# Stick-breaking attention: one 1408-column tile for a head's three score pieces

## The chip, the cores and the metric

The kernel runs on one core of a Trainium2 chip. The time is device microseconds of one execution; several executions are timed and the median is given. One execution was also recorded by the hardware profiler, and every row below comes from it.

## What is computed

The program is a two-layer diffusion block followed by a second block; the change concerns one part of the second: stick-breaking attention with 8 heads of 64 over 512 positions. Cut to that part, the reference is:

```python
def stick_breaking_attention(q, k, v):      # one block of queries
    z = einsum('bhqd,bhkd->bhqk', qb, kh) * scale
    mask = key_pos[None, :] < q_pos[:, None]
    log_1mb = where(mask, log_sigmoid(-z), 0.0)
    later = cumsum(log_1mb, axis=3, reverse=True) - log_1mb
    w = where(mask, exp(log_sigmoid(z) + later), 0.0)
    return einsum('bhqk,bhkd->bhqd', w, vh)
```

The kernel uses that -log_sigmoid(-z) is softplus(z) = max(z, 0) + ln(1 + exp(-|z|)).

## The kernel before

Scores stand with keys on the partitions. A head has four key tiles of 128; of the queries only those that can see the keys are kept, so key tile 0 has 512 columns, key tile 1 has 384, key tiles 2 and 3 have 256 each and share one bank. These three pieces (512, 384, 512 columns: indices 0, 1, 2) are three PSUM banks `Z`.

`sb_prep` (line 1624) makes a head's queries and keys: transposes (lines 1630 and 1634), a ScalarE copy (1637) and VectorE subtractions (1638, 1644). `sb_scores` (line 1651) issues 12 matmuls (lines 1656 to 1658) in the order of key tiles 2, 3, 1, 0, then for each piece in the order 2, 0, 1: the absolute value (ScalarE, 1664), exponential and logarithm (ScalarE through the helper of line 210, in place in tile `t`), max and add (VectorE, 1667), and `split` (lines 345 and 346): a cast to `hi` and a subtraction that gives `lo` (tiles `p`, VectorE). So a head has 9 ScalarE and 9 VectorE instructions here.

`sb_weights` (line 1753) adds the running sums to the scores in place: 20 matmuls (line 1760) with `hi` and `lo` of the pieces as the moving operand, beginning with key tile 3, which lies in piece 2; then three exponentials from `Z` to tiles `w`, which free the score banks. `sb_out` (line 1768) makes the output of a pair of heads from `w` (line 1774).

TensorE's instructions of the stage are in a scheduled order written out by hand:

```python
for h in range(9):
    if h < 8:
        W[h] = sb_weights(S.pop(h))
    ...
    if h and h % 2 == 0:
        sb_out(c, W)
    if h + 2 + N_PRE < 8:
        st[h + 2 + N_PRE] = sb_prep(h + 2 + N_PRE)
    if h + 2 < 8:
        S[h + 2] = sb_scores(st.pop(h + 2), sb_new)
```

So the scores of head h+2 come after the weights of head h, and before those of head h+1. Six PSUM banks hold the scores of two heads. The other engines are ordered by the scheduler, which also puts work of other lines between: sums of squares for norms (line 366), norm steps (384 to 399), and weight splits that are made ahead (345, 346). Head 0 is scored earlier, with tiles of other pools (`early_s`, line 1714); heads 1 to 7 use `sb_new` (line 1750). The pool "heads" lies on the right side of the on-chip memory, where the weight buffers lie before and after it; the loads of the next weights (line 268, SyncE's queue) wait until its tiles are free.

Of the kernel before, what the change touches and what calls it, by code (L numbers as in the profile page):

```python
# [10 lines left out]
F32 = mybir.dt.float32  # L11
F32R = mybir.dt.float32r
AF = mybir.ActivationFunctionType
ALU = mybir.AluOpType
# [4 lines left out]
P = 128  # L19
# [33 lines left out]
N_ARENA, N_TMP, N_TMP1, N_HS = 44, 4, 9, 6  # L53
N_H, N_H1, N_H2 = 12, 8, 12

N_AO, N_AP, N_E, N_RING, N_ST, N_SP, N_SW, N_TAB = 4, 12, 8, 16, 4, 12, 9, 8

N_MM, N_MA = 5, 6

# [22 lines left out]
def body(ctx: ExitStack, tc: tile.TileContext, a):  # L82
    nc = tc.nc
    T, V, A, G = nc.tensor, nc.vector, nc.scalar, nc.gpsimd

    def pool(es, name, bufs=1, side=None, space=None):
        kw = {} if space is None else {"space": space}
        return es.enter_context(tc.tile_pool(name=name, bufs=bufs, side=side, reuse_waits="tile", **kw))
# [12 lines left out]
    def nm(s):  # L101
        cnt[0] += 1
        return f"{s}{cnt[0]}"
# [17 lines left out]
    def ps(tag="mm"):  # L121
        return banks[tag].tile([P, 512], F32, tag=tag, name=nm("ps"))
# [10 lines left out]
    def s2(dt=F32, n=NX):  # L133

        return arena.tile([P, 512], dt, tag="a", name=nm("a"), bufs=N_ARENA)[:, :n]
# [35 lines left out]
    def col(n):  # L171
        o, w = COL[n]
        return cols[:, o:o + w]
# [17 lines left out]
    def f(x):  # L191
        return x.bitcast(F32)
# [10 lines left out]
    def act_fn(out, in_, func, **kw):  # L203
        s = TABLE[func]
        if s != table["set"]:
            load = A.preload_act_table_set(s)
            for u in table["users"]:
                after_(load, u)
            table.update(set=s, load=load, users=[])
        i = A.activation(out, in_, func, **kw)  # L210
        after_(i, table["load"])
        table["users"].append(i)
# [130 lines left out]
    def split(hi, lo, src, ce=A, se=V):  # L343

        last["copy"] = (ce.copy if ce is A else ce.tensor_copy)(hi, src)  # L345
        return se.tensor_tensor(lo, src, f(hi), ALU.subtract)  # L346
# [17 lines left out]
    def stat_add(acc, src, first, after=None):  # L364
        q = acc if first else tt(src.shape[1])
        i = A.activation(q, src, AF.Square)
        if after is not None:
            after_(i, after)
        if not first:
            V.tensor_tensor(acc, acc, q, ALU.add)  # L370
# [462 lines left out]
    for d in range(2):  # L833
        m = s2(F32R)
# [191 lines left out]
    for nme, gn in (("q", "qg"), ("k", "kg")):  # L1026
# [7 lines left out]
        for t in range(4):  # L1034
            for b in range(2):
                V.scalar_tensor_tensor(o5[:, t, :, b, :], s5[:, t, :, b, :], -1.0 if b == 0 else 1.0, g5[:, :, 1 - b, :],
                                       op0=ALU.mult, op1=ALU.mult)
# [173 lines left out]
    with tc.manual_schedule(engines={mybir.EngineType.PE}):  # L1211
        for n in range(-1, 25):
# [11 lines left out]
            new = {}  # L1224
# [399 lines left out]
    def sb_prep(h):  # L1624


        c, e = h // 2, h % 2
        q = ps2()
        for t in range(4):
            T.transpose(q[:, t * P:(t + 1) * P], qd[h // 4][t][:, (h % 4) * P:(h % 4 + 1) * P], ident)  # L1630
        if e == 0:
            k = ps2()
            for t in range(4):
                T.transpose(k[:, t * P:(t + 1) * P], kt[t][:, c * P:(c + 1) * P], ident)
        qh, ql = s2(F32R), s2(F32R)
        hs = slice(64 * e, 64 * e + 64)
        A.activation(qh, q, AF.Copy, scale=gqk)
        V.scalar_tensor_tensor(ql[hs], q[hs], gqk[hs], f(qh[hs]), op0=ALU.mult, op1=ALU.subtract)
        if e == 0:
            for i in range(2):  # L1640
                ks = keys[h + i] = s2(F32R)
                u, l = slice(64 * i, 64 * i + 64), slice(64 - 64 * i, 128 - 64 * i)
                A.copy(ks[u], k[u])
                V.tensor_tensor(ks[l], k[u], f(ks[u]), ALU.subtract)
        return qh, ql[hs], keys.pop(h), hs

    def sb_tile(x, k):

        return x[k][:, :NX - q0s[k]] if k < 2 else x[2][:, (k - 2) * 256:(k - 1) * 256]

    def sb_scores(st, new):
        qh, ql, ks, hs = st
        Z = [ps(), ps(), ps()]
        for k in (2, 3, 1, 0):
            z, s = sb_tile(Z, k), q0s[k]
            T.matmul(z, ks[:, k * P:(k + 1) * P], qh[:, s:], start=(k < 3), stop=False, skip_group_check=True)
            T.matmul(z, ks[hs, k * P:(k + 1) * P], ql[:, s:], start=False, stop=False, skip_group_check=True)  # L1657
            T.matmul(z[:, 0:256], identr, hide[:, 256:] if k == 3 else hide[:, :256], start=False, stop=True, skip_group_check=True)  # L1658
        TP = [None] * 3
        for k in (2, 0, 1):  # L1660
            n = (512, 384, 512)[k]
            z = Z[k][:, :n]
            hi, lo, b = new(F32R), new(F32R), new(F32)[:, :n]
            A.activation(b, z, AF.Abs)
            act_fn(b, b, AF.Exp, scale=-1.0)
            act_fn(b, b, AF.Ln, bias=1.0)
            V.scalar_tensor_tensor(b, z, 0.0, b, op0=ALU.max, op1=ALU.add)
            split(hi[:, :n], lo[:, :n], b, V)
            TP[k] = (hi, lo)
        return Z, [[x[i] for x in TP] for i in range(2)]  # L1670

    psum.close()
    psum = open_psum(6)
    st, S, W = {0: sb_prep(0), 1: sb_prep(1)}, {}, {}
# [40 lines left out]
    for h in range(SB_E):  # L1715
        S[h] = sb_scores(st[h], early_s)
# [18 lines left out]
    def stats(n_, tiles):  # L1735
        for c, x in enumerate(tiles):
            stat_add(accs[n_], x, c == 0)
# [6 lines left out]
    sb_es = ExitStack()  # L1744
    sbp = pool(sb_es, "heads", 2, side="right")

    def sb(tag, bufs, dt=F32R):
        return sbp.tile([P, 512], dt, tag=tag, name=nm(tag), bufs=bufs)

    def sb_new(dt):  # L1750
        return sb("t", N_ST, dt) if dt is F32 else sb("p", N_SP, dt)

    def sb_weights(st):
        Z, TP = st
        W = [None] * 3
        for k in range(3, -1, -1):
            z, s0 = sb_tile(Z, k), q0s[k]
            for k2 in range(k, 4):
                for x in TP:
                    T.matmul(z[:, q0s[k2] - s0:], ntri if k2 == k else nones, sb_tile(x, k2), start=False, stop=True, skip_group_check=True)  # L1760
            if k == 3:
                continue
            n = (512, 384, 512)[k]
            W[k] = sb("w", N_SW, F32)
            act_fn(W[k][:, :n], Z[k][:, :n], AF.Exp)
        return W

    def sb_out(c, W):

        o = ps2()  # L1770
        for k in range(4):
            for e in range(2):
                h = 2 * c + e
                T.matmul(o[64 * e:64 * e + 64, q0s[k]:], VV[k][:, h * 64:(h + 1) * 64], sb_tile(W[h], k), start=(k == 0), stop=(k == 3),  # L1774
                         tile_position=(0, 64 * e), skip_group_check=True)
        A.copy(OB[c], o)

    with tc.manual_schedule(engines={mybir.EngineType.PE}):
        for h in range(SB_E, 2):
            S[h] = sb_scores(st[h], sb_new)  # L1780
        for h in range(2, 2 + N_PRE):
            st[h] = sb_prep(h)
        for h in range(9):
            if h < 8:
                W[h] = sb_weights(S.pop(h))
            if h in ST_AT:
                stats(*(("c", OC), ("s", OS))[ST_AT.index(h)])
            if h and h % 2 == 0:
                c = h // 2 - 1
                sb_out(c, W)  # L1790
                if c == 0:
                    accs["b"] = s2()
                stat_add(accs["b"], OB[c], c == 0)
            if h + 2 + N_PRE < 8:
                st[h + 2 + N_PRE] = sb_prep(h + 2 + N_PRE)
            if h + 2 < 8:
                S[h + 2] = sb_scores(st.pop(h + 2), sb_new)
            if SG_SB <= h < SG_SB + 4:
                staged(h - SG_SB)
            if h in NORM_AT:  # L1800
                next(norms[NORM_AT.index(h) // 2])
# [36 lines left out]
    put, norm_xa, readyq, _, rbq = norm_late(X, act, acc, col("xag"))  # L1838
# [125 lines left out]
    put, done, readyf, _, rbf = norm_late(X, act, acc, col("ffng"))  # L1964
# [158 lines left out]
```

## Time and profile before

| | us |
|---|---|
| median of 3 runs | 2491.04 |
| lowest and highest run | 2489.52, 2492.58 |
| profiled execution, its own time | 2486.12 |
| its span, first to last instruction | 2484.3 |
| TensorE matmuls busy | 2426.6 |
| VectorE busy | 1586.3 |
| ScalarE busy | 915.9 |

In rows of the profile, PE is TensorE's matmuls and PEld its weight loads (they overlap), DVE is VectorE, ACT ScalarE, POOL GpSimd, SP SyncE. L1760 is line 1760 of the kernel; L210, L345 and L346 are lines of helpers, so the tile names tell whose work it is. A q behind an engine's name means its instruction queue. A row of the timeline may merge several instructions of one kind; its duration then runs from the first's start to the last's end. Matmul ends are modelled.

### The profile page before, as it was taken

The numbers are of one execution on the slowest core, as the hardware profiler recorded it, in microseconds if no ns is written. First come the engines' busy times: TensorE is split into PE (matmuls) and PEld (weight loads), VectorE is DVE, ScalarE is ACT, GpSimd is POOL, SyncE is SP. The second block draws the span as 40 slices with busy tenths as digits, with TensorE's granted clock in tenths as the row PEclk, the third lists the DMA queues.
The fourth block names the chain that finished last, engine by engine and source line by source line (L and its number), as shares of the span: only waits on it lengthen the run. The fifth ranks groups of instructions, "written<-read, shape, count | busy, mean of one in ns | idle before, by whom it ended". The sixth has DMA issues, their size and how long they took to land. (4 is left out here: it accounts for less than half of the span.)

```text
span 2484.3 us, 34508 instructions
## 1 busy us (share of the span) xinstructions
PE 2426.6 (98%) x13648; PEld 2007.2 (81%) x13648; DVE 1586.3 (64%) x3340; ACT 915.9 (37%) x1942; POOL 119.2 (5%) x172
## 2 busy tenths in 40 slices
PE   7999999999999999999999999999999999999999
PEld 6978889888888889964487888886877977888887
DVE  5689567666553336799877775488768666543442
ACT  4311563422212214456543232342486534322321
POOL 0000110000000000133200000000000000000000
PEclk9999999999999999999999999999999999999999
DMA  8535024234542122100232323333103522323322
GB/s 249 171 102 153 18 85 153 69 119 156 167 134 66 56 68 85 56 1 1 60 100 88 115 85 102 102 102 100 55 1 127 179 68 85 102 74 105 102 86 92
DMA packets 214769, 238.45 MB, mean 96 GB/s; under 512 B 10704, under 2 KB 166992, under 8 KB 214608
## 3 DMA queue, kind: packets, MB, share of 16 engines
q1 hardware_dynamic: 212880, 233.19, 29.2%
q10 hardware_dynamic: 1728, 3.07, 0.3%
q8 instruction: 107, 1.75, 0.3%
q14 instruction: 54, 0.44, 0.1%
HBM read 225.63 MB, written 8.39 MB: 94 GB/s over the span
## 5 line engine op out<-in xcount | busy, mean ns | idle before, releaser
L308 PE MATMUL ps<-a,whi 128*128 128x512 f32 (+1 forms) x3784 | 985.1, 355 | 4.9 <-DVE a L793 2.4
L308 PEld LDWEIGHTS ps<-a,whi 128*128 128x128 f32 x3784 | 641.5, 189 | 113.0 <-issue 7.2
L308 PE MATMUL ps<-a,wlo 128*128 128x512 f32 (+1 forms) x1980 | 641.2, 357 | 0.8 <-DVE wlo L346 0.8
L345 ACT CAST whi<-wst 128x528 fp32r<-128x528 f32 (+3 forms) x611 | 337.9, 610 | 593.0 <-PE ps L308 519.3
L308 PE MATMUL ps<-h,whi 128*128 128x512 f32 (+1 forms) x1776 | 456.3, 352 | 2.8 <-DVE h L345 2.7
L346 DVE TENSOR_TENSOR wlo<-wst,whi 128x528 fp32r<-128x528 f32 (+3 forms) x611 | 390.3, 674 | 76.3 <-ACT whi L345 75.2
L308 PEld LDWEIGHTS ps<-a,wlo 128*128 128x128 f32 x1980 | 346.4, 189 | 56.0 <-issue 2.3
L308 PEld LDWEIGHTS ps<-h,whi 128*128 128x128 f32 x1776 | 294.9, 188 | 52.9 <-DVE h L345 6.5
L308 PE MATMUL ps<-h,wlo 128*128 128x512 f32 (+1 forms) x800 | 237.8, 347 | 0.0
L564 DVE SCALAR_TENSOR_TENSOR a<-ps,mods,a 128x512 f32<-128x512 f32 (+1 forms) x200 | 121.9, 638 | 153.2 <-PE ps L308 152.6
L338 PE MATMUL ps<-whi,a 128*128 128x256 f32 (+1 forms) x1024 | 191.2, 285 | 0.6 <-ACT a L1577 0.6
L338 PEld LDWEIGHTS ps<-whi,a 128*128 128x128 f32 x1024 | 160.8, 191 | 11.3 <-issue 7.9
L491 DVE SCALAR_TENSOR_TENSOR mac<-ada,sc,mac 128x512 f32<-128x512 f32 x224 | 157.3, 744 | 19.2 <-DMA ada<-ada_w 17.9
L308 PEld LDWEIGHTS ps<-h,wlo 128*128 128x128 f32 x800 | 133.8, 188 | 19.5
L338 PE MATMUL ps<-wlo,a 128*128 128x256 f32 (+1 forms) x512 | 145.3, 285 | 0.5 <-DVE wlo L346 0.5
L553 ACT ACTIVATE t<-ps 128x512 f32<-128x512 f32 x60 | 35.9, 598 | 285.5 <-PE ps L308 273.0
L345 DVE CAST h<-t 128x512 fp32r<-128x512 f32 x60 | 25.5, 425 | 147.1 <-ACT t L555 147.1
L338 PEld LDWEIGHTS ps<-wlo,a 128*128 128x128 f32 x512 | 97.6, 191 | 2.1 <-issue 1.1
L350 POOL TENSOR_TENSOR sm<-sm,mhalf 128x2 f32<-128x2 f32 (+2 forms) x27 | 28.6, 1058 | 969.0 <-DVE sm L386 965.8
L210 ACT ACTIVATE p<-ps 128x512 f32<-128x512 f32 x96 | 53.7, 596 | 41.1 <-PE ps L1147 33.2
L1127 DVE TENSOR_REDUCE mx<-ps 128x1 f32<-128x512 f32 (+1 forms) x128 | 62.8, 546 | 6.0 <-PE ps L1126 5.7
L2008 DVE TENSOR_TENSOR a<-a,ps 128x512 f32<-128x512 f32 x16 | 11.0, 688 | 80.2 <-PE ps L308 80.2
(433 smaller groups left out, 2970.7 us busy)
## 6 DMA issues: line engine op xcount, KB each, us to landing
wst<-mlp_w SPq DMA_DIRECT2D x64, 1024.0 KB, 5.1
ada<-ada_w SPq DMA_DIRECT2D x80, 512.0 KB, 4.0
wst<-ffn_w_in SPq DMA_DIRECT2D x20, 1024.0 KB, 5.0
wst<-ffn_w_out SPq DMA_DIRECT2D x16, 704.0 KB, 4.2
wst<-hyb_w_in SPq DMA_DIRECT2D x10, 1024.0 KB, 5.6
wst<-w_in SPq DMA_DIRECT2D x9, 1024.0 KB, 5.1
a<-ada_w SPq DMA_DIRECT2D x32, 256.0 KB, 5.0
wst<-att_w_in SPq DMA_DIRECT2D x6, 1024.0 KB, 5.0
```

What stands on the lines that cost most here:

```text
L210: i = A.activation(out, in_, func, **kw)
L308: T.matmul(p, w(k, slice(m, m + P)), tiles[t][i // 2][:, s:s + n], start=(k == k0 and i == 0), stop=(k == k1 and i == 2))
L338: T.matmul(p, tiles[i // 2][:, s:s + P], (wl if i == 1 else wh)(k, slice(0, n)), start=(k == 0 and i == 0), stop=(k == KC - 1 and i == 2))
L345: last["copy"] = (ce.copy if ce is A else ce.tensor_copy)(hi, src)
L346: return se.tensor_tensor(lo, src, f(hi), ALU.subtract)
L350: G.tensor_tensor(r, v, mhalf[:, :n], ALU.pow)
L491: V.scalar_tensor_tensor(m, x, s, m, op0=ALU.mult, op1=ALU.add)
L553: A.activation(r, p, AF.Relu)
L564: V.scalar_tensor_tensor(xs, p, mod(l, 5)(c, v), xs, op0=ALU.mult, op1=ALU.add)
L1127: V.tensor_reduce(MX[:, e, t, i:i + 1], z, AX.X, ALU.max)
L2008: V.tensor_tensor(xs, xs, p, ALU.add)
```

## The change

For heads 1 to 7 the three pieces are placed side by side in one tile of 1408 columns for each of `b`, `hi` and `lo`. Absolute value and max-and-add stay three instructions (their source is three banks); exponential, logarithm, cast and subtraction become one each. The weight matmuls read slices of the wide tiles. The buffers become 2 tiles `t` of 1408 columns in place of 4 of 512, and 6 tiles `p` of 1408 in place of 12 of 512. Head 0 goes through the same code with one piece at a time, as before. The orders of TensorE and of the pieces are the same.

```diff
-N_AO, N_AP, N_E, N_RING, N_ST, N_SP, N_SW, N_TAB = 4, 12, 8, 16, 4, 12, 9, 8
+N_AO, N_AP, N_E, N_RING, N_ST, N_SP, N_SW, N_TAB = 4, 12, 8, 16, 2, 6, 9, 8
+SB_N = 1408
...
-        TP = [None] * 3
-        for k in (2, 0, 1):
-            n = (512, 384, 512)[k]
-            z = Z[k][:, :n]
-            hi, lo, b = new(F32R), new(F32R), new(F32)[:, :n]
-            A.activation(b, z, AF.Abs)
+        TP = [[None] * 3 for _ in range(2)]
+        for ks in ((2, 0, 1),) if new is None else ((2,), (0,), (1,)):
+            ns = [(512, 384, 512)[k] for k in ks]
+            n = sum(ns)
+            hi, lo, b = (sb(t, m, dt, SB_N) if new is None else new(dt)[:, :n] for t, m, dt in (("p", N_SP, F32R), ("p", N_SP, F32R), ("t", N_ST, F32)))
+            at = {k: slice(sum(ns[:i]), sum(ns[:i + 1])) for i, k in enumerate(ks)}
+            for k in ks:
+                A.activation(b[:, at[k]], Z[k][:, :(512, 384, 512)[k]], AF.Abs)
             act_fn(b, b, AF.Exp, scale=-1.0)
             act_fn(b, b, AF.Ln, bias=1.0)
-            V.scalar_tensor_tensor(b, z, 0.0, b, op0=ALU.max, op1=ALU.add)
-            split(hi[:, :n], lo[:, :n], b, V)
-            TP[k] = (hi, lo)
-        return Z, [[x[i] for x in TP] for i in range(2)]
+            for k in ks:
+                V.scalar_tensor_tensor(b[:, at[k]], Z[k][:, :(512, 384, 512)[k]], 0.0, b[:, at[k]], op0=ALU.max, op1=ALU.add)
+            split(hi, lo, b, V)
+            for k in ks:
+                TP[0][k], TP[1][k] = hi[:, at[k]], lo[:, at[k]]
+        return Z, TP
...
-            S[h] = sb_scores(st[h], sb_new)
+            S[h] = sb_scores(st[h], None)
...
-                S[h + 2] = sb_scores(st.pop(h + 2), sb_new)
+                S[h + 2] = sb_scores(st.pop(h + 2), None)
```

## Rows read from the trace of the kernel before

**Rows 1.** The page, busy us, share of the span and instructions of each engine.

```profile
PE 2426.6 (98%) x13648; PEld 2007.2 (81%) x13648; DVE 1586.3 (64%) x3340; ACT 915.9 (37%) x1942; POOL 119.2 (5%) x172
```

**Rows 2.** Busy time by stretch: length, engines' busy us, granted clock, DMA share, GB/s.

```profile
1814.00:1823.00 9.00, 7.32 (x33) 6.68 (x34) 6.83 (x13) 6.56 (x15) 0.00 (x0) 0.62 0.00 1
1823.00:1863.90 40.90, 40.89 (x229) 29.47 (x227) 30.91 (x55) 37.60 (x75) 1.01 (x1) 1.00 0.00 1
...
1866.00:1873.00 7.00, 6.95 (x19) 4.61 (x20) 3.07 (x7) 3.67 (x8) 0.00 (x0) 0.53 0.00 0
```

**Rows 3.** Timeline of TensorE: start, us, line, operation, tiles [idle before, releaser].

```profile
1787.86 0.50 PE L308 MATMUL ps<-a,whi 128*128 128x512 f32 x1 [1.07 <-ACT a L345]
...
1816.32 1.11 PE L1630 MATMUL ps<-kst,a 128*128 128x128 f32 x4 [1.68 <-ACT a L1712]
...
1826.21 0.39 PE L1658 MATMUL ps<-hide,identr 128*128 128x256 f32 x1
...
1833.65 0.64 PE L1760 MATMUL ps<-p,ntri 128*128 128x256 f32 x4
...
1842.66 0.38 PE L1658 MATMUL ps<-hide,identr 128*128 128x256 f32 x1
...
1850.58 0.39 PE L1658 MATMUL ps<-hide,identr 128*128 128x256 f32 x1
1850.80 0.64 PE L1760 MATMUL ps<-p,ntri 128*128 128x256 f32 x4
...
1860.49 1.04 PE L1760 MATMUL ps<-p,ntri 128*128 128x256 f32 x4
...
1866.05 0.38 PE L1656 MATMUL ps<-a,a 128*128 128x256 f32 x1 [2.16 <-ACT w L210]
...
1871.21 0.58 PE L1658 MATMUL ps<-hide,identr 128*128 128x256 f32 x1
...
1878.67 0.72 PE L1760 MATMUL ps<-p,ntri 128*128 128x256 f32 x4
...
1879.65 0.62 PE L308 MATMUL ps<-a,a 128*128 128x512 f32 x2
...
1896.23 0.62 PE L308 MATMUL ps<-a,whi 128*128 128x512 f32 x2
```

**Rows 4.** Instruction groups by shape, 1814 to 1884 us: count, busy us, mean ns, idle before.

```profile
L210 ACT ACTIVATE t<-t 128x512 f32<-128x512 f32 x28 | 16.6, 636 | 0.1
...
L346 DVE TENSOR_TENSOR p<-t,p 128x512 fp32r<-128x512 f32 x14 | 9.6, 685 | 0.2
...
L210 ACT ACTIVATE t<-t 128x384 f32<-128x384 f32 x14 | 7.5, 539 | 0.0
L345 DVE CAST p<-t 128x512 fp32r<-128x512 f32 x14 | 5.9, 422 | 0.2
...
L346 DVE TENSOR_TENSOR p<-t,p 128x384 fp32r<-128x384 f32 x7 | 3.8, 549 | 0.1
...
L345 DVE CAST p<-t 128x384 fp32r<-128x384 f32 x7 | 2.5, 352 | 0.0
```

**Rows 5.** Timeline of ScalarE, the same columns.

```profile
1846.03 0.59 ACT L210 ACTIVATE w<-ps 128x512 f32<-128x512 f32 x1
...
1851.00 0.60 ACT L1664 ACTIVATE t<-ps 128x512 f32<-128x512 f32 x1 [1.23 <-DVE p L346]
...
1860.07 1.12 ACT L1664 ACTIVATE t<-ps 128x512 f32<-128x512 f32 x2
...
1865.35 1.52 ACT L210 ACTIVATE w<-ps 128x512 f32<-128x512 f32 x3
```

**Rows 6.** Timeline of VectorE, the same columns.

```profile
1849.81 0.73 DVE L1638 SCALAR_TENSOR_TENSOR a<-ps,gqk,a 64x512 fp32r<-64x512 f32 x1
...
1854.48 1.29 DVE L1667 SCALAR_TENSOR_TENSOR t<-ps,t 128x512 f32<-128x512 f32 x2
```

**Rows 7.** Waits of the load queue, 1800 to 1900 us: us in total, times, longest.

```profile
SPq L268 <- PE ps L1760: 9.0, 2, 6.8
```

More of the change, by code (lines that the diff above doesn't have):

```diff
@@ L1745, in body, with sb @@
     sbp = pool(sb_es, "heads", 2, side="right")
[L1747 to L1751, printed above, removed]
+    def sb(tag, bufs, dt=F32R, n=512):
+        return sbp.tile([P, n], dt, tag=tag, name=nm(tag), bufs=bufs)
     def sb_weights(st):
```

## The prediction

> **What bounds the kernel now.** I read the page's busy line first: TensorE is busy for 98% of the span [rows 1], so an edit on other engines counts only where TensorE waits for them. The change touches one stage, stick-breaking attention, from 1814 us to about 1885 us. I read it by stretches next [rows 2]: from 1823 to 1863.9 us TensorE is busy 40.89 of 40.90 us, ScalarE 37.60, VectorE 30.91. TensorE sets the pace there, ScalarE runs at 92% beside it. The stage has two weak places. Before 1816.32 TensorE stood still for 1.68 us, until a ScalarE copy released a PSUM bank; before 1866.05 it stood still for 2.16 us, until an exponential of the weights (tile w) released the bank of a score tile [rows 3]. [...]
>
> Then I read when a head's scores are done and when they are needed, because TensorE's order is written out by hand and can't be changed by the scheduler. Call E the end of a head's last score matmul (line 1658) and W the start of its weight matmuls (line 1760), which read hi and lo. Between the two TensorE works for other heads; that stretch is the cover under which ScalarE and VectorE must make hi and lo. From rows 3: head 2 has E 1826.60 and W 1833.65, a cover of 7.05 us. Head 4: 1843.04 to 1850.80, 7.76. Head 5: 1850.97 to 1860.49, 9.52. Head 7: 1871.79 to 1878.67, 6.88. Even heads have the short covers, since the output matmuls of a pair (line 1774) stand in the odd heads' cover; head 7 has no further scores behind it.
>
> **The change part by part.** *Fewer, longer instructions.* Heads 1 to 7 change; head 0 keeps its three pieces. Per head two exponentials and two logarithms, two casts and two subtractions go: 8 instructions, 56 in all. Length by rows 4: ScalarE takes 636 ns for 512 columns in place and 539 for 384, so 0.76 ns a column, and 1408 columns are 636 + 896 x 0.76 = 1.32 us. The cast is 422 and 352, 0.55 ns a column: 0.91 us. The subtraction is 685 and 549, 1.06 ns a column: 1.64 us. ScalarE's busy time for the two functions falls from 2 x (636 + 636 + 539) = 3.62 to 2.64 us a head, VectorE's for cast and subtraction from 3.12 to 2.55 us. Both run beside a TensorE that is never idle from 1823 to 1863.9 us [rows 2]: worth nothing there by itself. [...]
>
> *The chain after E gets longer.* Before, the three pieces run through ScalarE and VectorE as a pipeline, and W may begin on the first piece. After, the exponential waits for all three absolute values, VectorE for the whole logarithm, and W for the whole subtraction. Piece 0's scores are the last on TensorE, so after E there follow: the absolute values of pieces 0 and 1, 0.98 (two of 512 columns take 1.12 us [rows 5], times 896/1024); exponential and logarithm 2 x 1.32; max-and-add of three pieces, 1.29 for two [rows 6] and 0.55 for 384 columns, as the subtraction of that size [rows 4]; cast 0.91; subtraction 1.64. Sum 8.0 us. Two things can slip in. A weight exponential of the head before, 0.59, was put between two steps of the chain at 1846.03 [rows 5]; half of it is hidden in the wait of logarithm on exponential, so I take 0.3. A query subtraction (line 1638), 0.73, stood between a cast and its subtraction at 1849.81 [rows 6]; I leave it out of the value and keep it for the bound. The chain is 8.3 us, between 8.0 and 8.0 + 0.59 + 0.73 = 9.3.
>
> *Covers less chain.* Head 2: 8.3 - 7.05 = 1.25 us of new idle time. Head 4: 0.55. Heads 1, 3 and 5: none; head 5 with 9.52 is the tightest of those I quote. Head 7: 8.3 - 6.88 = 1.4; two matmuls of the following projection already stand inside its weight matmuls at 1879.65 [rows 3], and a longer hole may take more of them, so I take 1.0, between 0 and 2.4. Head 6: its W stands behind the scores of head 7, which start after the halt, at 1866.05, and end at 1871.79 [rows 3]; its chain, 8.3 us from 1860.07 [rows 5], is done at 1868.4; nothing.
>
> *The halt at 1866.05.* The weight exponentials of head 5 began at 1865.35, after a queue of ScalarE work that began at 1860.07 [rows 5]. Merged steps may let them go earlier or block them; the nearest row is the halt itself, so I take no change, between +1 us and the whole of it gone: 2.16 us and the low spell, 7.0 x 0.47 = 3.3 us [rows 2], together -5.5.
>
> *Buffers.* Four narrow b tiles become two wide ones. The wait of 1.23 us for a b tile at 1851.00 [rows 5] goes; it lay under head 5's cover, so it is worth nothing. What is late next there is the chain itself. Six wide hi/lo tiles hold three heads instead of two, so no wait is added. The heads' pool lies where the next weights are loaded: the load queue waited 9.0 us in two waits for weight matmuls (line 1760) to release it [rows 7], and a new layout moves that; TensorE first reads those weights at 1896.23 [rows 3], 17.6 us after head 7's W, so zero; if that cover were gone, what the load is late by would show in front of that row.
>
> **Sum.** 1.25 + 0.55 + 1.0 = +2.8 us. The profiled execution took 2486.12 us for its span of 2484.3 us and lies 4.9 us under the median of the runs, 2491.04. So 2488.9 for that execution, 2493.8 us for the runs. About 0.2% (5 us) is what a measurement of this kernel can tell from no change, so this is "the same": +0.11%.
>
> **Rivals.** *TensorE's clock falls in the new holes (slower).* With the chain at 9.3 us the idle times are 2.25 (head 2), 1.55 (head 4) and 2.4 us (head 7), 6.2 in all. The two halts of 1.68 and 2.16 us went with a low clock, the one of 1.07 did not; so it decides between 1.07 and 1.68 us of idle time, before head 2's or head 7's weight matmuls. One low spell costs 3.3 us: +9.5, 2500.5 us; with two 2503.8. For it: both rows had this price in this stage. Against: at 8.3 us head 2's hole is 1.25 us. Chance 0.33.
>
> *The old halts go (faster).* With fewer entries in ScalarE's queue the scheduler may put the copy that was waited for at 1816.32, and head 5's weight exponentials, ahead of the long steps. The first is worth 1.68 + 9.0 x 0.38 = 5.1 us at most, the second 5.5; with the new holes +2.8 both together give -7.8, 2483.2 us; either alone is inside "the same". For: after the change ScalarE has nothing else of the chain to do until a head's last scores come. Against: a long step also blocks the queue for longer. Chance 0.15.
>
> *ScalarE paces the stage (faster).* If it did, its saving of 0.98 us a head would be the gain: 7 x 0.98 = 6.9, 2484.1 us at most. For: 92% busy. Against: TensorE's 40.89 of 40.90 us. [...] Chance 0.07.
>
> *Nothing shows.* W needs hi first and lo after it, and the scheduler may put the chain ahead of everything; at 8.0 us only head 2 is short, by 0.95, and head 7's hole is filled: +1.2 with head 4's 0.24, 2492.2 us. This is inside "the same".
>
> **Numbers.** Same 0.45 (forecast and "nothing shows"), slower 0.33, faster 0.15 + 0.07 = 0.22. Range 2484 to 2502 us: down to the two faster rivals, up past the case with one low spell. The forecast's own range, with its bounds of 8.0 and 9.3 us and no change of clock, is 2492 to 2497.
>
> **What would show it.** In the changed trace: 7 exponentials and 7 logarithms of 1408 columns at about 1.32 us, casts at 0.91, subtractions at 1.64; TensorE idle before line 1760 for heads 2, 4 and 7 on a VectorE subtraction, and nowhere new for odd heads 3 and 5; the halts at 1816 and 1866 us still there. I am wrong if those holes are missing, if a halt of old is gone, or if the clock is low in a stretch in which it was full.

## The result and the profile after

| | us |
|---|---|
| after, median of 4 runs (lowest, highest) | 2517.17 (2514.18, 2519.80) |
| before, median of 4 runs | 2490.28 (2485.81, 2492.58) |
| ratio, 95% interval | 1.0105 (1.0086 to 1.0123) |
| profiled execution of after, its span | 2515.63, 2513.9 |

The change costs 1.05%, some 26 us (the two medians lie 26.9 us apart). I had forecast no measurable difference. In the rows of after all lines have moved down a little: the helpers of lines 210, 345 and 346 are lines 212, 347 and 348, score matmuls are 1658 to 1660, absolute values 1669, max-and-add 1673, weight matmuls 1764, output matmuls 1778, query and key subtractions 1640 and 1646.

The page's busy line of after, and the wide instructions in its groups by shape (1820 to 1905 us; count, busy us, mean ns, idle before):

```profile
PE 2439.9 (97%) x13648; PEld 2014.5 (80%) x13648; DVE 1584.5 (63%) x3312; ACT 915.9 (36%) x1914; POOL 118.9 (5%) x172
```

```profile
L212 ACT ACTIVATE t<-t 128x1408 f32<-128x1408 f32 x14 | 19.3, 1377 | 0.2
L348 DVE TENSOR_TENSOR p<-t,p 128x1408 fp32r<-128x1408 f32 x7 | 11.4, 1625 | 0.2
...
L347 DVE CAST p<-t 128x1408 fp32r<-128x1408 f32 x7 | 6.2, 885 | 0.1
```

The instructions did become what the diff says: 28 fewer on VectorE and 28 fewer on ScalarE than in [rows 1]. Their lengths were priced well: 1.38 us measured for 1.32, 0.89 for 0.91, 1.63 for 1.64. So the loss is not in their lengths. It is in when they run.

TensorE issues the score and weight matmuls of the stage in the same order in every run, so the same two stretches can be cut out of each by count: *the stage*, 400 matmuls from head 0's first score matmul on, which reach a few behind the last outputs, and *behind*, the next 200, which reach into the projection w_out. Only matmuls of the following projection and its statistics change places, among the last 50 of the 400: the two that stood inside head 7's weight matmuls [rows 3] come later in after. The windows view, of before and then of after (length, busy us of PE, PEld, DVE, ACT, POOL, granted clock, DMA share, GB/s):

```profile
1805.08:1887.93 82.85, 79.01 (x403) 56.97 (x401) 58.18 (x105) 68.14 (x138) 2.19 (x2) 0.92 0.08 26
1887.93:1929.05 41.12, 40.00 (x202) 32.80 (x200) 35.72 (x71) 21.93 (x45) 2.14 (x2) 1.00 0.48 167
```

```profile
1812.68:1909.18 96.50, 84.02 (x402) 60.55 (x401) 55.35 (x77) 67.30 (x107) 2.01 (x2) 0.86 0.07 22
1909.18:1958.62 49.44, 43.16 (x202) 34.90 (x202) 36.05 (x71) 22.89 (x47) 2.14 (x2) 0.93 0.41 139
```

Length minus PE's busy time is TensorE's idle time. The stage grew by 13.65 us: 8.64 more of idle time (12.48 for 3.84) and 5.01 more of busy time, for the same matmuls at a mean clock of 0.86 instead of 0.92. Behind it another 8.32 us went, 5.16 idle and 3.16 of slower matmuls. I had not looked for a loss there at all. Together 22.0 of the 26 us.

The rest lies ahead of the stage, or in the scatter. The stage began 7.6 us later in this execution than in the one I had read, with the same order of instructions on every engine up to there. A second execution of before began it 5.5 us later than the first, and a kernel with wide tiles (e_act) 0.5 us earlier (the table below). So that part lies within what executions vary by, and the trace that I forecast from was a quick one.

**The halts of the stage.** TensorE's timeline in after, the halts of 0.4 us and more, with the last score matmul of heads 2 and 4 (start, us, line, tiles, count, [idle before, releaser]):

```profile
1824.80 0.66 PE L1632 MATMUL ps<-kst,a 128*128 128x128 f32 x4 [2.57 <-ACT a L1719]
...
1831.35 0.36 PE L1658 MATMUL ps<-a,a 128*128 128x256 f32 x1 [0.60 <-DVE a L1646]
...
1834.53 0.39 PE L1660 MATMUL ps<-hide,identr 128*128 128x256 f32 x1
...
1842.38 0.40 PE L1764 MATMUL ps<-p,ntri 128*128 128x256 f32 x1 [0.45 <-DVE p L347]
1845.46 1.01 PE L1764 MATMUL ps<-p,ntri 128*128 128x256 f32 x3 [2.68 <-DVE p L348]
...
1856.25 0.39 PE L1660 MATMUL ps<-hide,identr 128*128 128x256 f32 x1
...
1865.07 0.39 PE L1764 MATMUL ps<-p,ntri 128*128 128x256 f32 x1 [0.52 <-DVE p L347]
1868.08 1.01 PE L1764 MATMUL ps<-p,ntri 128*128 128x256 f32 x3 [2.62 <-DVE p L348]
...
1885.03 0.38 PE L1658 MATMUL ps<-a,a 128*128 128x256 f32 x1 [1.57 <-ACT w L212]
...
1891.35 1.00 PE L1764 MATMUL ps<-p,ntri 128*128 128x256 f32 x3 [1.48 <-DVE p L348]
```

The holes of heads 2 and 4 are where they were forecast, but 3.1 us each (0.45 + 2.68, and 0.52 + 2.62 for head 4) instead of 1.25 and 0.55. Head 6 has one of 1.48 us; head 7 has none. A new one of 0.60 us stands ahead of head 2's scores. The two old halts [rows 3] stayed, one longer (2.57 for 1.68), one shorter (1.57 for 2.16). Behind each of the two large new holes the same matmuls of 256 columns merge to 1.01 us for three, where four took 0.64 before [rows 3]. The granted clock behind them is 0.50 (from 1845.50 to 1849.30 and from 1868.10 to 1873.00 us); where the four took 0.64, it was 1.00 [rows 2].

**Head 2's chain.** ScalarE, then VectorE, in after:

```profile
1834.95 0.60 ACT L1669 ACTIVATE t<-ps 128x512 f32<-128x512 f32 x1 [0.48 <-PE ps L1660]
1835.44 0.62 ACT L368 ACTIVATE a<-a 128x512 f32<-128x512 f32 x1
1835.96 1.37 ACT L212 ACTIVATE t<-t 128x1408 f32<-128x1408 f32 x1
1837.24 0.58 ACT L212 ACTIVATE w<-ps 128x512 f32<-128x512 f32 x1
1837.71 1.38 ACT L212 ACTIVATE t<-t 128x1408 f32<-128x1408 f32 x1
...
1839.12 1.75 DVE L1673 SCALAR_TENSOR_TENSOR t<-ps,t 128x512 f32<-128x512 f32 x3 [2.33 <-ACT t L212]
1840.79 0.73 DVE L1640 SCALAR_TENSOR_TENSOR a<-ps,gqk,a 64x512 fp32r<-64x512 f32 x1
1841.45 0.88 DVE L347 CAST p<-t 128x1408 fp32r<-128x1408 f32 x1
1843.06 0.68 DVE L1646 TENSOR_TENSOR a<-ps,a 64x512 fp32r<-64x512 f32 x1 [0.74 <-ACT a L1645]
1843.78 1.63 DVE L348 TENSOR_TENSOR p<-t,p 128x1408 fp32r<-128x1408 f32 x1
```

E is 1834.92, and the subtraction ends at 1845.41: 10.5 us, where I had 8.3. Start to start, the chain's own steps take 7.4 us. Other heads' work takes 3.1: a square for a norm (0.52), a weight exponential (0.47), a query subtraction (0.66), and between the cast and the subtraction 0.73 us of waiting for ScalarE's key cast and 0.72 for the key subtraction that waited for it. The wide subtraction needed none of that; it stood behind it in VectorE's order.

The same chain in before ends with these subtractions, of head 2 and of head 4 (piece 1, the last in the order):

```profile
1832.73 0.54 DVE L346 TENSOR_TENSOR p<-t,p 128x384 fp32r<-128x384 f32 x1
...
1850.47 0.54 DVE L346 TENSOR_TENSOR p<-t,p 128x384 fp32r<-128x384 f32 x1
```

From E in [rows 3] that is 6.7 us in head 2 and 8.0 in head 4, against covers of 7.05 and 7.76. Head 2 had 0.4 us to spare. Head 4's last remainder came 0.2 us after W, without a halt, since W begins with another piece. So there was hardly any room before the change, and head 2's chain grew by 3.8 us.

### The profile page after: what moved, and what is told of

Its sections match the earlier page's. It is cut to its first block, busy times and chain, and to the rows that moved or that the text cites. A ratio compares the mean times of both kernels' runs of the same rounds, so it can differ in the third digit from the quotient of the medians.

```text
span 2513.9 us, 34447 instructions
## 1 busy us (share of the span) xinstructions
PE 2439.9 (97%) x13648; PEld 2014.5 (80%) x13648; DVE 1584.5 (63%) x3312; ACT 915.9 (36%) x1914; POOL 118.9 (5%) x172
## 3 DMA queue, kind: packets, MB, share of 16 engines
q8 instruction: 107, 1.75, 0.3%
## 5 line engine op out<-in xcount | busy, mean ns | idle before, releaser
L348 DVE TENSOR_TENSOR wlo<-wst,whi 128x528 fp32r<-128x528 f32 (+3 forms) x611 | 391.1, 677 | 76.9 <-ACT whi L347 75.8
```

## The experiments

Edits are against the changed kernel unless said otherwise; where its lines are packed so that the numbers of before hold, rows show those. The table has for every profiled run where the stage began, and for both stretches length, idle time (length minus PE busy) and mean clock, all from the windows view. The expectations count the stage in a shorter way, only to the start of the last pair's output matmuls; that length, from the timeline, is the column "to outputs".

| run | stage begins | to outputs | stage: us, idle, clock | behind: us, idle, clock |
|---|---|---|---|---|
| before | 1805.08 | 77.92 | 82.85, 3.84, 0.92 | 41.12, 1.12, 1.00 |
| before again (ctl_before) | 1810.59 | 79.19 | 84.12, 3.84, 0.90 | 41.08, 1.11, 1.00 |
| after | 1812.68 | 91.48 | 96.50, 12.48, 0.86 | 49.44, 6.28, 0.93 |
| after again (after_again) | 1813.09 | 91.77 | 96.79, 12.36, 0.84 | 49.39, 6.30, 0.93 |
| wide tiles alone (e_buf) | 1809.12 | 79.38 | 85.24, 4.07, 0.90 | 48.67, 6.12, 0.93 |
| wide on ScalarE alone (e_act) | 1804.54 | 92.58 | 97.37, 13.27, 0.88 | 49.58, 6.31, 0.93 |
| wide on VectorE alone (e_dve) | 1806.93 | 76.88 | 81.69, 3.29, 0.94 | 48.81, 6.15, 0.93 |
| two pieces + one (e_21) | 1804.82 | 76.67 | 80.92, 4.02, 0.96 | 49.64, 6.93, 0.93 |
| wide in heads 1, 3, 5 (e_odd) | 1816.99 | 82.30 | 87.20, 6.62, 0.90 | 49.17, 6.25, 0.93 |
| keys behind (after_keys) | 1812.48 | 90.03 | 95.05, 8.98, 0.84 | 49.09, 6.30, 0.93 |
| w_out pinned (after_order) | 1807.86 | 91.94 | 96.96, 12.41, 0.84 | 49.90, 7.31, 0.93 |
| norm late (after_late) | 1812.71 | 91.45 | 96.47, 12.37, 0.86 | 40.73, 0.71, 1.00 |
| before, norm late (before_late) | 1805.99 | 78.24 | 83.17, 3.82, 0.92 | 42.33, 1.74, 1.00 |
| combination (dve_late_pw) | 1810.31 | 76.45 | 81.25, 2.25, 0.94 | 40.92, 0.80, 1.00 |

**Both kernels again.** First, how much of all this is scatter.

> The changed program itself once more, nothing altered. It measures what an execution varies by, above all the stretch ahead of the stage, where the changed kernel was 7.6 us later than the one before although TensorE's instructions there stand in the same order. Theory (the early lag is the execution's, not the change's): the lag at the stage's start will differ from +7.6 us by several us, while the stage again takes 91.5 us from head 0's first score matmul to the last output matmuls (77.9 before). Rival (the early lag belongs to the program): +7 to +8 us at the stage's start again.

> The kernel before itself once more, nothing altered, for a second trace of it. Theory (the early lag is the execution's): from 600 to 960 us it will be several us later than the first trace of it, with TensorE's instructions in the same order, and the stage takes 77.9 us again. Rival (the early lag belongs to the changed program): the first 1800 us agree with the first trace within 1.5 us.

After again took 2516.27 us, before again 2492.86. The stage repeats within 1.3 us, the stretch behind within 0.05. Where the stage begins doesn't. After again lay 8.0 us behind the first trace of before, as the rival said and not the theory; before again lay 5.5 us behind it, as the theory said. Over all runs the beginning varies by 12.5 us, in no order with the edit. That scatter is left unexplained, and whether the changed program itself begins later is not shown.

**Halves of the change.** Three kernels keep the wide tiles; the first does every operation by pieces in them, the second joins only ScalarE's two functions, the third only VectorE's cast and subtraction.

```diff
 # e_buf
+for k in ks:
+    c = b[:, at[k]]
+    A.activation(c, Z[k][...], AF.Abs); act_fn(c, c, AF.Exp, scale=-1.0); act_fn(c, c, AF.Ln, bias=1.0)
+    V.scalar_tensor_tensor(c, Z[k][...], 0.0, c, op0=ALU.max, op1=ALU.add)
+    split(hi[:, at[k]], lo[:, at[k]], c, V)
 # e_act: abs, exp and ln as in the changed kernel, then
+for k in ks:
+    V.scalar_tensor_tensor(b[:, at[k]], Z[k][...], 0.0, b[:, at[k]], op0=ALU.max, op1=ALU.add)
+    split(hi[:, at[k]], lo[:, at[k]], b[:, at[k]], V)
 # e_dve: abs to max-and-add as in e_buf, then
+split(hi, lo, b, V)
```

> Wide tiles and the halved buffer counts stay, but every piece keeps its own exponential, logarithm, cast and subtraction in slices of them. Theory (the long steps make the loss): the stage takes 78 us as before (76 to 81), the whole within 0.2% of the kernel before apart from what the order behind the stage does. Rival (buffers and their place in memory make it): the stage takes 88 us or more, the whole stays about 25 us slower.

> ScalarE's half alone: one exponential and one logarithm of 1408 columns, but max-and-add, cast and subtraction piece by piece. Theory (chain after the last scores against the cover, both engines' long steps add to it): between the two kernels, the stage 81 to 87 us, TensorE idle before the weight matmuls of heads 2 and 4 by about 1 us each instead of 3. Rival (VectorE's wide subtraction, behind which or in front of which a key subtraction waits, makes all of it): the stage as before, 78 us. Other rival (ScalarE's long steps make all of it): 90 us or more.

> VectorE's half alone: three exponentials and logarithms piece by piece, one cast and one subtraction of 1408 columns. Theory (both add to the chain): the stage 81 to 87 us. Rival (VectorE's wide steps make all of it): 90 us or more with the holes before heads 2 and 4 as in the changed kernel, 2.6 us each. Other rival (ScalarE's make all): 78 us.

Times (before in the same batch 2488.68): e_buf 2495.06, ratio 1.0027 (1.0013 to 1.0041); e_act 2512.08, 1.0090 (1.0072 to 1.0109); e_dve 2493.21, 1.0022 (1.0009 to 1.0035). By stretches it is plainer. The joined exponential and logarithm alone bring the whole loss of the stage (97.37 us), though VectorE's pieces are short again. The joined cast and subtraction alone bring none (81.69). Both theories of a loss shared by the two engines failed: 92.6 and 76.9 us to the outputs, not 81 to 87. And the loss behind the stage, 7.5 to 8.5 us, is in all three, also where no instruction is wide. With ScalarE by pieces head 2's chain fits its cover again (heads 4 and 7 still wait, 0.5 and 0.7 us). VectorE in e_dve, where max-and-add is line 1666, and TensorE's head 2 there (its E is 1828.45):

```profile
1828.06 0.39 PE L1658 MATMUL ps<-hide,identr 128*128 128x256 f32 x1
...
1835.43 0.64 PE L1760 MATMUL ps<-p,ntri 128*128 128x256 f32 x4
...
1831.08 1.16 DVE L1666 SCALAR_TENSOR_TENSOR t<-ps,t 128x512 f32<-128x512 f32 x2 [0.76 <-ACT t L210]
1832.27 0.89 DVE L345 CAST p<-t 128x1408 fp32r<-128x1408 f32 x1
1833.20 1.63 DVE L346 TENSOR_TENSOR p<-t,p 128x1408 fp32r<-128x1408 f32 x1
```

From E to the end of the subtraction are 6.4 us here, against a cover of 7.0: no hole. The first piece's max-and-add ran at 1829.63, while ScalarE was still at the others, and nothing slipped in behind the last. In after VectorE waits 2.33 us for the whole logarithm (the chain's rows above) and only then begins all of its work.

**Two pieces joined, the last alone.** Pieces 2 and 1, whose scores come first, are joined, and piece 0, whose scores come last, stays by itself on both engines.

```diff
+for g in ((2, 1), (0,)):
+    c = slice(at[g[0]].start, at[g[-1]].stop)
+    for k in g: A.activation(b[:, at[k]], Z[k][...], AF.Abs)
+    act_fn(b[:, c], b[:, c], AF.Exp, scale=-1.0); act_fn(b[:, c], b[:, c], AF.Ln, bias=1.0)
+    for k in g: V.scalar_tensor_tensor(b[:, at[k]], Z[k][...], 0.0, b[:, at[k]], op0=ALU.max, op1=ALU.add)
+    split(hi[:, c], lo[:, c], b[:, c], V)
```

> Pieces 2 and 1, whose scores TensorE makes first, merged in all steps (896 columns), piece 0 by itself; wide tiles as in the changed kernel. Theory (the loss is what follows the last scores, E, before the weight matmuls may start): only piece 0's short steps follow E (0.60 + 0.64 + 0.64 + 0.69 + 0.42 + 0.69 = 3.7 us), under every cover, so the stage takes 77 to 80 us. Rival (long steps as such, which block ScalarE's queue for the weight exponentials and casts): 83 us or more.

The stage takes 80.92 us, and no weight matmul waits; the run took 2492.3 us, with the loss behind the stage still in it. The stage is 1.9 us shorter than in before, by the clock (0.96) and not by idle time (4.02). So joining pieces doesn't cost by itself. But the theory's reason isn't what the trace shows. TensorE, ScalarE and VectorE in that run, head 2:

```profile
1825.57 0.58 PE L1658 MATMUL ps<-hide,identr 128*128 128x256 f32 x1
...
1826.68 2.82 ACT L210 ACTIVATE t<-t 128x896 f32<-128x896 f32 x4
...
1831.55 1.69 DVE L346 TENSOR_TENSOR p<-t,p 128x896 fp32r<-128x896 f32 x2
```

E is 1826.15 and the last subtraction ends at 1833.24: a chain of 7.1 us, not 3.7, because the joined exponential too ran behind E. That is close to the 7.4 us of the chain's own steps in after. What is missing is the other work: no instruction of another head stands between these steps.

**Wide in the odd heads only.** They have the longer covers, up to 9.52 us. The first branch is that of e_buf, the second that of the changed kernel.

```diff
+if len(ks) == 1 or not mrg[0]:
+    for k in ks:
+        ...
+else:
+    ...
+mrg[0] = h + 2 in (1, 3, 5); S[h + 2] = sb_scores(st.pop(h + 2), None)
```

> All steps merged in heads 1, 3 and 5, piece by piece in heads 2, 4, 6 and 7; wide tiles throughout. Theory (even heads have the short covers): no hole before the weight matmuls of heads 2 and 4, the stage takes 77 to 81 us. Rival (each merged head costs the same): three sevenths of 13.6 us, 84 us.

2510.29 us, of which 11.9 is a late beginning of the stage; the stage itself lost 4.35. To the outputs it took 82.3 us, above the 77 to 81 of the theory. Heads 2 and 4 have no hole now, but head 3 got one, from a wait I had not priced. TensorE and VectorE of that run (its weight matmuls are line 1767):

```profile
1855.89 0.95 PE L384 MATMUL ps<-ones,a 128*128 128x1 f32 x8
...
1858.63 1.01 PE L1767 MATMUL ps<-p,ntri 128*128 128x256 f32 x3 [1.56 <-DVE p L346]
...
1853.40 0.89 DVE L345 CAST p<-t 128x1408 fp32r<-128x1408 f32 x1
1856.88 0.16 DVE L386 TENSOR_SCALAR sm<-ps 128x4 f32<-128x4 f32 x1 [2.58 <-PE ps L384]
1856.96 1.62 DVE L346 TENSOR_TENSOR p<-t,p 128x1408 fp32r<-128x1408 f32 x1
```

The cast was done at 1854.29. The subtraction could have followed, but a norm step of 0.16 us stood ahead of it and waited 2.58 us for statistics that TensorE makes behind the scores.

**Query and key subtractions behind the wide one.** The two that stood in head 2's chain are ordered behind the latest wide subtraction.

```diff
-V.scalar_tensor_tensor(ql[hs], q[hs], ...)
+i_ = V.scalar_tensor_tensor(ql[hs], q[hs], ...); 'sb' in last and after_(i_, last['sb'])
-V.tensor_tensor(ks[l], k[u], f(ks[u]), ALU.subtract)
+i_ = V.tensor_tensor(ks[l], k[u], f(ks[u]), ALU.subtract); 'sb' in last and after_(i_, last['sb'])
-split(hi, lo, b, V)
+last['sb'] = split(hi, lo, b, V)
```

> The changed kernel, with VectorE's query and key subtractions of the next heads ordered behind the wide subtraction of the head in hand, so that they no longer stand between its cast and its subtraction. Theory (the chain after the last score matmul is longer than its own instructions because those two stand in it): head 2's chain falls from 10.5 us to about 8.4 and that of head 4 alike, the two halts before their weight matmuls shrink from about 3.1 us each to about 1, and the stage from 91.5 us to 84 to 88. Rival (the halt is not set by the chain, or the delayed keys make the next scores late): the halts stay within 0.5 us of 3.1, or a new one of 1 us or more stands before the next head's score matmuls, and the stage stays above 90 us.

2514.38 us against 2492.71, ratio 1.0091 (1.0069 to 1.0112). The first half of the theory held: head 2's chain is 8.5 us (E 1836.45 to 1844.99), and the halts fell to about what was said. Head 4's chain fell only to 10.4 (E 1856.79, subtraction 1865.58 to 1867.21), since ScalarE's logarithm was late. The second half failed: to the outputs the stage took 90.0 us, not 84 to 88, which is the bound of its rival. Of 3.5 us less idle time 2.05 came back as slower matmuls. TensorE and its stretches in that run:

```profile
1845.04 1.01 PE L1760 MATMUL ps<-p,ntri 128*128 128x256 f32 x3 [1.20 <-DVE p L346]
...
1856.62 1.17 PE L384 MATMUL ps<-ones,a 128*128 128x1 f32 x8
...
1867.26 0.87 PE L1760 MATMUL ps<-p,ntri 128*128 128x256 f32 x3 [0.87 <-DVE p L346]
```

```profile
1843.60:1843.84 0.24, 0.24 (x1) 0.00 (x0) 0.24 (x1) 0.24 (x1) 0.00 (x0) 0.50 0.00 0
...
1845.00:1850.00 5.00, 4.96 (x19) 4.76 (x19) 3.23 (x6) 4.17 (x6) 0.00 (x0) 0.50 0.01 2
...
1857.00:1861.00 4.00, 4.00 (x20) 3.96 (x20) 0.85 (x2) 2.10 (x3) 1.01 (x1) 0.57 0.02 4
```

Behind head 2's halt of 1.20 us the clock was 0.50 for 5.0 us; behind that of 2.68 in after it was 0.50 for 3.8 us (1845.50 to 1849.30). But the first of the stretches above, with TensorE busy, lies just ahead of the halt, which began at 1843.84: the clock was low before it. So shortening the holes gave little here, and that the holes themselves lower the clock is not shown.

**Behind the stage.** In after, TensorE and then VectorE in w_out:

```profile
1934.95 0.62 PE L310 MATMUL ps<-a,whi 128*128 128x256 f32 x3 [1.38 <-ACT whi L347]
1936.66 0.38 PE L310 MATMUL ps<-a,whi 128*128 128x256 f32 x1 [1.08 <-DVE a L1836]
1939.94 0.79 PE L310 MATMUL ps<-a,wlo 128*128 128x512 f32 x1 [2.90 <-DVE wlo L348]
...
1939.19 3.66 DVE L348 TENSOR_TENSOR wlo<-wst,whi 128x528 fp32r<-128x528 f32 x6
```

The projection's weights come in four units, the first of them made inside the stage. The last two remainders (wlo) of the third unit are made at 1939.19, with those of the fourth, behind the steps of the memory norm, which run on VectorE from 1925.95 to 1936, and a few more. In before the third unit's are all made ahead of that norm's first step at 1905.65:

```profile
1904.72 0.63 DVE L346 TENSOR_TENSOR wlo<-wst,whi 128x464 fp32r<-128x464 f32 x1
1905.65 0.16 DVE L386 TENSOR_SCALAR sm<-ps 128x2 f32<-128x2 f32 x1 [0.29 <-PE ps L384]
```

TensorE's order differs there too: four 256-wide matmuls of the last unit went ahead. One kernel ties TensorE to the old order; the next moves the norm (statistics and scaling) behind the projection's weight loads; the third is that move in the kernel before.

```diff
 # after_order, in fm(): each matmul behind the unit's first
+i_ = T.matmul(p, w(k, slice(m, m + P)), ...); pinned(i_, chain, us)
 # after_late, before_late
-    rb = stat_end(accm, D)
-    for c in range(KC):
-        norm_apply(M[c], rb, col("memg")[:, c:c + 1], None, *actm[c])
+    def mem_norm():
+        yield
+        rb = stat_end(accm, D)
+        for c in range(KC): norm_apply(M[c], rb, col("memg")[:, c:c + 1], None, *actm[c])
+    fillers.append(mem_norm())
...
-       then=a["xa_wk"][:, 0:256])
+       then=a["xa_wk"][:, 0:256]); finish()
```

> The changed kernel with one thing pinned: in the projection behind the stage (w_out) TensorE may not begin the last weight unit before the one ahead of it is issued. In every kernel with wide tiles so far four matmuls of the last unit stand in front of the second half of the unit before, and TensorE then waits 1.38, 1.1 and 2.9 us; the other engines' order is not touched. Theory (the order of those four matmuls makes the loss behind the stage): the 8.4 us behind the stage go, the stage stays at 91.5 us, about 2509 us in all. Rival (the weights are late anyway, since the wide tiles release their memory later): the same halt a little later, 2517 us again.

> The changed kernel, with the memory norm (its statistics and its scaling) moved from ahead of the w_out projection's third weight unit to behind the projection's weight loads, so that the last weight-remainder subtractions on VectorE no longer stand behind it. Theory (the 8.3 us lost behind the stage are those subtractions, late because the norm's VectorE steps stand ahead of them): the halts of 1.38, 1.08 and 2.90 us in w_out go, matmul for matmul the lag stops growing between the last output matmul and the w_out matmuls (0 to 2 us instead of 8.3), the stage still loses about 13.6 us against the kernel before, and the time is about 2509 us (ratio 1.0075 to the kernel before, between 1.005 and 1.009). Rival (the third unit's weights are late in any order, since their load or their conversion waits for something else): TensorE still waits for the remainder tile in w_out, and the time stays at the changed kernel's 2516 us (ratio 1.0105).

> The kernel before with the same move of the memory norm behind w_out's weight loads: a control. Theory: there the remainders are done before the norm's statistics begin, so there is nothing to win: ratio 0.999 to 1.002. Rival (the norm's late place is a gain of its own in any kernel): 3 us or more faster (ratio under 0.999).

Tied, TensorE has one halt for the remainder tile instead of three, and the same loss, against the theory: 2514.48 us, ratio 1.0106 (1.0087 to 1.0125). In that run the projection is line 314 and the remainder's helper 352:

```profile
1935.58 0.80 PE L314 MATMUL ps<-a,wlo 128*128 128x512 f32 x1 [6.37 <-DVE wlo L352]
```

With the norm late the loss is gone: 40.73 us and clock 1.00, as in before; 2505.77 us, ratio 1.0055 (1.0039 to 1.0072). What is left, 0.55% or 13.7 us, is what the stage lost by the traces, 13.6. The same move in before changes nothing that can be told (1.0009, 0.9996 to 1.0022). So the place of the norm makes the loss behind the stage: in VectorE's order, and for the halt of 1.38 us in ScalarE's, where casts of the norm stood ahead of the fourth unit's. Why the scheduler chose another order when the tiles became wide, no run shows.

**A combination.** VectorE wide, ScalarE by pieces (e_dve), the norm late, and the copy behind the halt of 1.68 us [rows 3] moved to VectorE.

```diff
-        A.copy(OC[c], items[0][1])
+        V.tensor_copy(OC[c], items[0][1])
```

> A version meant to beat both: the pieces in one tile, absolute value, exponential and logarithm piece by piece as before, cast and subtraction once over 1408 columns, the memory norm behind w_out's weight loads, and the copy that ends conv_pw2 ahead of the stage moved from ScalarE to VectorE. Theory: the stage loses nothing (as with the VectorE half alone, 1.2 us less than before), the halt of 1.68 us at the stage's first mix goes with the 1 to 2 us of low clock behind it, and the 7.7 us behind the stage go: 2484 to 2489 us (ratio 0.998 to 1.0). Rival (VectorE, with the copy added, is late with the first heads' sums): a new halt of 1.5 us or more in heads 0 to 2, and 2490 us or more.

2490.35 us, ratio 0.9994 (0.9981 to 1.0008): no worse than before, not measurably better, and 1.4 us above the 2484 to 2489 that I had expected. The halt fell from 1.68 to 0.64 us, that of 2.16 to 0.38, and the stage takes 1.6 us less; but TensorE's busy time in it stayed at 79.0 us, so the low clock wasn't won back. No version here beats the kernel before by more than can be measured.

## Why the prediction was wrong

*What bounds the kernel* was right: TensorE, busy for 97% of the span in after, sets the pace, and 56 instructions saved elsewhere gave nothing.

*Fewer, longer instructions*: right in each length, to 0.06 us. The saving that I priced from them, 0.98 us a head on ScalarE, is not there: ScalarE is busy for 915.9 us in both kernels, and in the stage for 67.30 us after 68.14. I had added up durations that overlap: in [rows 5] one absolute value takes 0.60 us and two take 1.12. Breaking up exponential and logarithm alone takes the stage from 96.50 to 81.69 us (e_dve), and VectorE's wide pair, which stays in that run, costs nothing there. So the long instructions cost time on the engine whose work the other waits for, not on both.

*The chain after E*: the right mechanism, in heads 2 and 4, with one term mis-sized. This is the step that failed. "Two things can slip in" was 0.3 us, at most 1.32; it measured 3.1 in head 2. The chain's own steps came to 7.4, below my 8.0. Taking half of a weight exponential as hidden was about right: with one of 0.58 us between them, head 2's logarithm began 1.75 us behind its exponential, and in head 7, with none, 1.41, so it added 0.34. I had counted the duration of what could stand between two steps, once each, from places where the pieces still ran as a pipeline. What stands there also waits for its own inputs (0.73 us of waiting here, 2.58 in e_odd). With VectorE's part of it moved away (after_keys) the chain fell from 10.5 to 8.5 us. Nor had I read the chain of the kernel before, which left next to no room.

*Covers less chain*: the covers hadn't moved (head 2: 7.0 us). With 10.5, 11.4 and 11.5 us of chain in heads 2, 4 and 6 the holes are 3.1, 3.1 and 1.5. Head 6 I had put at nothing from a chain of 8.3; its subtraction stood behind one that waited 1.91 us for a cast on ScalarE. Head 7, put at 1.0, had none.

*The halt at 1866.05* I left as it was; it shrank by 0.6, while the earlier one grew by 0.9: its copy, at 1824.18, now stands behind an exponential of 1.38 us that began at 1822.90. The rival in which the old halts go is refuted.

*Buffers*: "zero" failed, by 8.3 us. I asked whether the weights' load would be late, and looked at the first read of the first weights. The load wasn't the trouble; the conversion of the third unit was, because VectorE's order changed some 30 us behind the last wide instruction. This is the second term that failed, put at nothing.

*The rivals*: the one that came nearest is the low clock in new holes. Its priced case had one spell of 3.3 us; the stage lost 5.0 to the clock and 8.6 to idle time. I gave it 0.33, and it alone would still have missed the loss behind the stage. That the holes set the clock, as it said, is not shown (next but one section). ScalarE as the bound is refuted: it has 28 instructions less and slightly less to do, and the stage is longer.

*The sum*, +2.8 us forecast: +13.65 in the stage, +8.32 behind it, and some 4 us that lie in the scatter ahead.

## What to carry over

Joining the operations of a head's three pieces made VectorE wait here for the last piece's input and the longest instructions (2.33 us in head 2, for a logarithm of 1.38); price the chain from the last input to the first use, with everything that stands in order on the same engines, its own waits included, and read first how much room the chain has now. Joining only the early pieces (e_21, one run) or only on the last engine of the chain (e_dve) opened no large hole here (idle time of the stage 4.02 and 3.29 us, where before had 3.84). The change of tile sizes came with another order of VectorE's work some 30 us behind the last wide instruction and with 8.32 us of loss there, so compare the instruction orders there before putting it at zero.

## What was unexpected of the hardware

The granted clock fell where TensorE had not halted. In the run with the keys behind it was 0.57 from 1857 to 1861 us, with TensorE busy 4.00 of 4.00 us (the rows above); the last halt of 0.4 us or more lay 12 us back, and just ahead stood eight one-column statistics matmuls. In before_late, whose stage is that of the kernel before, it was 0.50 for 3.3 us behind 23.3 us without idle time, at the same place behind eight such matmuls:

```profile
1820.50:1843.80 23.30, 23.30 (x132) 17.00 (x132) 16.91 (x32) 20.88 (x41) 0.00 (x0) 1.00 0.00 1
1843.90:1847.20 3.30, 3.30 (x14) 3.11 (x14) 2.94 (x5) 3.30 (x9) 0.93 (x1) 0.50 0.02 5
```

In before it was 1.00 there [rows 2]. In after it was already low in head 2 ahead of the halt of 2.68 us, which began at 1842.78, behind one of only 0.45:

```profile
1842.62:1842.77 0.15, 0.15 (x1) 0.00 (x0) 0.00 (x0) 0.15 (x1) 0.00 (x0) 0.50 0.00 0
```

On the other hand, a halt of 1.07 us ahead of the stage [rows 3] had no sequel: in before the granted clock was 1.00 from its end at 1787.86 to 1795 us. So in these runs the length of the halt, on which my rival's deciding point rested, doesn't tell whether the clock falls. What does, they leave open.
